# Linear attention and block 2's value products from unrounded fp32 operands, both head pairs at once, and weights in units of four tiles

## Chip, cores and metric

One core of one Trainium2 chip runs the whole program. The metric is the device time of one execution in microseconds (us); lower is better. TensorE is called PE (PEld is its weight load), VectorE DVE, ScalarE ACT, GpSimd POOL and SyncE SP.

## The reference

Two transformer blocks run one after the other on x of 512 positions by 1024 channels, all in fp32. Cut to what matters:

```python
# block 1: block attention (8 heads of 64) and differential attention (4 heads), gates, feed-forward
merged = sigmoid(ga) * (ya @ w_branch_a) + sigmoid(gb) * (yb @ w_branch_b)
x = x + rms_norm(merged @ w_out, g)
f = (silu(h @ w_gate) * (h @ w_up)) @ w_down          # 2816 wide

# block 2: linear attention with decay (4 heads, keys 64, values 128) beside 8 dilated heads of 64
b = cumsum(log_a)                                     # per chunk of 64
scores = einsum('bhik,bhjk,bhijk->bhij', q, k, exp(b_i - b_j))   # causal
o = (q * exp(b)) @ state + scores @ v
state = state * exp(b_last) + (k * exp(b_last - b)).T @ v
p = softmax(q @ k.T / 8 + bias);  y = p @ v           # dilated heads
x = x + g1 * (concat(rms_norm(o) * silu(r), y) @ w_out)
x = x + g2 * ((silu(conv(h @ w_up)) * conv(h @ w_up)) @ w_down)
```

Before the first line of block 2, a modulation vector is made from `w_ada` (48 tiles of 128 by 1024).

## The kernel before, in words

**Products.** Activations lie transposed, 128 channels by 512 positions. A weight tile is 128 by 128; there are 1760. Full precision comes from three products of rounded operands (type fp32r): each operand is split into a rounded high part and the rounded rest, and `mm3` adds high-high, high-low and low-high. Weights are split on the chip: `_raw` starts the transfer of eight tiles (128x1024) on SP into one of two buffers `wraw`, `_split` makes `whi` (a cast, on ACT or DVE) and `wlo` (a subtraction, on DVE) from a half of it, four tiles, and asks for the next transfer; `wt` hands out tiles and splits up to three halves ahead. A buffer is free once both its halves are split.

**Order.** A planner (`Rec`) holds a model of the costs of all engines, places every operation at its modelled time, and `play` emits them in that order; so every operation has the line of `play` (L311). On each engine the order is fixed: an operation that waits holds all that stand behind it. `either` lets the planner choose between two engines (`copy`: ACT or DVE; `both` and `aside`: DVE or POOL). `pump` mixes tasks (attention heads, norms) with dense work (projection tiles, `mtile`): a task that can go is taken first, dense work fills, and some dense work is held back until a head is done (`d_qk`, `d_gr`).

**Stages in the order of time.** Block 1's projections and attention (`block1_mix`) to about 320 us; there `e_b` evacuates branch b: a product into `gb`, the add of both branches into x, the split. Then `block1_rest`: a bridge over `w_out`, the gate and up products (`e_gate`, `e_up`: `g`, `sg`, `u`, `ah`, `al`), with `modulate` beside them: POOL starts the transfer of a tile of `w_ada` into one of two buffers, DVE multiplies and sums it (`junk`). Per gate and up pair two or three of these are done. Then the bridge over `w_down`, `block2_mix`, a bridge over `w_out2`, and block 2's feed-forward.

**Linear attention** (`gla`, for a pair p of heads). The decay is factored over levels: for distances below 128 seven levels (64 to 1), `near`, each an exponential `E` and products of E with k and q, put into zero-padded operands `pad` (high and low parts of both), four blocks of 128 by 128 on PE, and a predicated copy into the scores `A`. Distances of 128 and 256 are `far`. `turn` makes the probabilities' parts `pth` and `ptl` of a block, and `av` multiplies them with the values' parts. The resource `gla` lets one pair in at a time. `dilated` does a dilated head: scores, softmax, transposes, `att_v`.

## Time and profile before

| | |
|---|---|
| median of 3 runs | 1486.25 us (1485.28 to 1488.97) |
| the profiled execution | 1485.08 us; its span 1483.3 us |
| PE, DVE, ACT, POOL busy | 1417.5, 967.2, 674.5, 117.8 us |
| mean granted PE clock | 0.987 |
| transfers | 220 of 512 KB for weights, 48 of 512 KB for `w_ada` |

The span runs from the first to the last instruction of the profiled execution; launch and end lie around it. A busy time is a sum over an engine's instructions; an idle time is put down to what ended it. The granted clock is 1 at 2.4 GHz and 0.5 at 1.2 GHz. A true fp32 product is two matmul rows in the trace, a rounded one and a transpose one.

### The profile page before, as it was taken

What the parts mean: (1) busy time and instruction counts of PE and PEld (TensorE: products, weight loads), DVE (VectorE), ACT (ScalarE), POOL (GpSimd) and SP (SyncE); (2) the same over time, 40 slices, a digit from 0 to 9 for tenths busy, and PEclk for the clock granted to TensorE, in tenths of its full rate; (3) what the DMA queues carried; (4) which work ended last, traced back from release to release, by engine and by line L of the source; (5) the groups of instructions that cost most, each with busy time, mean ns of one, the idle gap of its engine ahead of it and who ended that gap; (6) DMA issues with size and microseconds to landing.
All of it is one profiled execution on the core that took longest, in us unless ns stands there. A gap on an engine that the chain in (4) does not pass through costs nothing.

```text
span 1483.3 us, 19294 instructions
## 1 busy us (share of the span) xinstructions
PE 1417.5 (96%) x7168; PEld 1183.1 (80%) x7168; DVE 967.2 (65%) x1906; ACT 674.5 (45%) x1333; POOL 117.8 (8%) x152
## 2 busy tenths in 40 slices
PE   8999999999999888899999999889999999999999
PEld 6888888877988666688899777768798788888887
DVE  7877766765775665562457688866866777776322
ACT  5665555543533222232335566756547344443221
POOL 0100000000110110000004012111000000000000
PEclk9999999999999999999999999899999999999999
DMA  4222222335235554533334111122332334433432
GB/s 171 71 72 71 73 84 86 86 107 163 86 91 180 181 172 160 197 114 101 91 122 133 53 58 53 33 65 70 94 110 61 102 112 128 128 88 112 121 114 64
DMA packets 44894, 154.89 MB, mean 104 GB/s; under 512 B 5104, under 2 KB 5760, under 8 KB 44800
## 3 DMA queue, kind: packets, MB, share of 16 engines
q1 hardware_dynamic: 36464, 124.16, 27.2%
q0 software_dynamic: 8192, 29.36, 6.6%
q8 instruction: 56, 0.92, 0.3%
q14 instruction: 38, 0.31, 0.1%
q10 hardware_dynamic: 144, 0.14, 0.0%
HBM read 149.45 MB, written 4.19 MB: 104 GB/s over the span
## 4 chain that ended last, share of the span: by engine, by line
PE 78%; DVE 9%; DMA 5%; ACT 4%; issue 3%; POOL 0%; SPq 0%; ACTq 0%; DVEq 0%; POOLq 0%
PE mm L311 62%; PE s L311 8%; DMA wraw<-w 5%; PE y L311 3%; PE pt L311 3%; PE pc L311 1%; DVE junk L311 1%; DVE wlo L311 1%; DVE u L311 1%; ACT ah L311 1%; DVE E L311 1%; DVE p L311 1%; ACT whi L311 1%; ACT E L311 0%; DVE hl L311 0%
## 5 line engine op out<-in xcount | busy, mean ns | idle before, releaser
L311 PE MATMUL mm<-hh,whi 128*128 128x512 f32 x1096 | 438.9, 400 | 24.7 <-DVE u L311 13.6
L311 PE MATMUL mm<-hh,wlo 128*128 128x512 f32 x1096 | 431.2, 393 | 12.8 <-DVE wlo L311 12.8
L311 PE MATMUL mm<-hl,whi 128*128 128x512 f32 x1096 | 429.5, 392 | 0.0
L311 DVE TENSOR_TENSOR wlo<-wraw,whi 128x512 fp32r<-128x512 f32 x401 | 272.3, 692 | 202.0 <-ACT whi L311 191.6
L311 ACT CAST whi<-wraw 128x512 fp32r<-128x512 f32 x358 | 217.7, 619 | 363.2 <-PE mm L311 172.7
L311 PEld LDWEIGHTS mm<-hh,whi 128*128 128x128 f32 x1096 | 207.3, 189 | 69.2 <-ACT whi L311 17.7
L311 PEld LDWEIGHTS mm<-hh,wlo 128*128 128x128 f32 x1096 | 207.2, 189 | 63.3 <-DVE wlo L311 18.9
L311 PEld LDWEIGHTS mm<-hl,whi 128*128 128x128 f32 x1096 | 207.6, 189 | 39.4 <-DVE hl L311 0.5
L311 PE MATMUL mm<-ah,whi 128*128 128x512 f32 (+1 forms) x296 | 111.9, 378 | 0.1
L311 PE MATMUL mm<-al,whi 128*128 128x512 f32 (+1 forms) x296 | 111.8, 378 | 0.0
L311 PE MATMUL mm<-ah,wlo 128*128 128x512 f32 (+1 forms) x296 | 111.8, 378 | 0.0
L311 DVE SCALAR_TENSOR_TENSOR junk<-p,p 128x1024 bf16<-128x1024 f32 x48 | 58.7, 1222 | 8.9 <-DMA p<-w_ada 8.4
L311 PEld LDWEIGHTS mm<-ah,whi 128*128 128x128 f32 x296 | 55.7, 188 | 10.7 <-DVE u L311 0.5
L311 PEld LDWEIGHTS mm<-al,whi 128*128 128x128 f32 x296 | 55.7, 188 | 10.3
L311 PEld LDWEIGHTS mm<-ah,wlo 128*128 128x128 f32 x296 | 55.7, 188 | 10.3
L311 POOL TENSOR_TENSOR rr<-rv,mhalf 128x4 f32<-128x4 f32 (+2 forms) x26 | 31.5, 1210 | 404.4 <-DVE rv L311 404.4
L311 POOL DMA_DIRECT2D p<-w_ada x48 | 26.1, 543 | 414.6 <-DVE junk L311 346.6
L311 DVE TENSOR_TENSOR ptl<-pt,pth 128x256 fp32r<-128x256 f32 (+3 forms) x92 | 42.3, 479 | 23.7 <-ACT pth L311 22.2
L311 ACT ACTIVATE p<-p,nm 128x128 f32<-128x128 f32 (+1 forms) x96 | 52.8, 552 | 6.7 <-DVE nm L311 6.6
L311 ACT CAST pth<-pt 128x256 fp32r<-128x256 f32 (+3 forms) x84 | 32.6, 412 | 45.7 <-PE pt L311 45.7
L311 DVE CUSTOM_DVE_ANT_0 p<-s,bias 128x128 f32<-128x128 f32 (+1 forms) x96 | 44.4, 488 | 7.4 <-PE s L311 6.3
L311 ACT ACTIVATE sg<-g 128x512 f32<-128x512 f32 x22 | 13.9, 632 | 56.6 <-DVE g L311 56.6
(498 smaller groups left out, 2407.5 us busy)
## 6 DMA issues: line engine op xcount, KB each, us to landing
wraw<-w SPq DMA_DIRECT2D x220, 512.0 KB, 3.6
p<-w_ada POOLq DMA_DIRECT2D x48, 512.0 KB, 4.6
x<-xT SPq DMA_DIRECT2D x8, 256.0 KB, 5.5
x<-xT POOLq DMA_DIRECT2D x8, 256.0 KB, 3.1
xd<-x SPq DMA_DIRECT2D x8, 256.0 KB, 4.5
x<-xd POOLq DMA_DIRECT2D x8, 256.0 KB, 3.0
outT<-x SPq DMA_DIRECT2D x7, 256.0 KB, 2.7
p<-c SPq DMA_DIRECT2D x2, 512.0 KB, 3.9
```

What stands on the lines that cost most here:

```text
L311: i = getattr(getattr(nc, eng), op)(*(real(v) for v in a), **{k: real(v) for k, v in kw.items()})
```

## The change

Weights come in units of four tiles (256 KB) into four buffers; each unit is split by itself and asks for the fourth unit after it. In block 2 the values are kept unrounded (`v_whole`), the probabilities too (`att_whole`, `turn`), and the near and far products take one fp32 product for three rounded ones; E is multiplied straight into the padded operands, for which each pair of heads has its own set; both pairs may be in `gla` at once, and `calm` holds a near step back while the planner's DVE or ACT lane is full more than 2 us ahead. The near products' multiplications by q, and those of `far`, may go to POOL. The heads of block 1 stay as they were. The planner now counts 310 and not 380 GB/s for a transfer; the add in `e_b` may go to POOL (`aside`); a bridge without ready columns begins with the banks `s`; the lambda load of block 1 is issued no earlier than its turn, and block 1's first squares come after the splits. The first four units are asked for between the tiles of x. The rest of the diff is names of tiles and sizes.

```diff
 NTILES = 976 + 784
-NCHUNK = -(-NTILES // 8)
+NHALF = NTILES // 4
+NRAW = 4
...
+CALM = 2.0
...
+PTB = 2
+EB = 3
+VB = 2
...
-            return (0.6 if eng == "gpsimd" else 0.43), b / 380e3, ()
+            return (0.6 if eng == "gpsimd" else 0.43), b / 310e3, ()
...
-        self.limit = 2 * NCHUNK
-        self.res = {"prob": 3, "pv": 1, "gla": 1, "sc": 1, "sq": 1, "v": 1}
+        self.limit = NHALF
+        self.res = {"prob": 3, "pv": 1, "gla": 2, "sc": 1, "sq": 1, "v": 1}
...
+    def calm(self, *vs):
+        n = self.when(*vs)
+        n.calm = True
+        return n
...
-        return max([t.ready] + [self.bank_at(b) for b in t.banks])
+        w = max([t.ready] + [self.bank_at(b) for b in t.banks])
+        if t.calm:
+            w = max(w, *(self.nc.lane[n].end() - CALM for n in ("vector", "scalar")))
+        return w
...
-    def _raw(self, c):
-        if c < NCHUNK and c not in self.raws:
-            raw = self.t(self.wp, [128, 1024], F32, "wraw", 2)
-            self.nc.sync.dma_start(out=raw, in_=self.a["w"][c])
-            self.raws[c] = raw
+    def _raw(self, h):
+        if h < NHALF and h not in self.raws:
+            raw = self.t(self.wp, [128, 512], F32, "wraw", NRAW)
+            self.nc.sync.dma_start(out=raw, in_=self.a["w"][h])
+            self.raws[h] = raw
     def _split(self, h):
-        c, half = divmod(h, 2)
-        if c >= NCHUNK or h in self.chunks:
+        if h >= NHALF or h in self.chunks:
             return
-        self._raw(c)
-        raw = self.raws[c][:, 512 * half:512 * half + 512]
+        self._raw(h)
+        raw = self.raws[h]
         if h in self.keep:
             w = self.keep.pop(h)
             hi, lo = self.hpair(w) if isinstance(w, int) else (self.W(*t) for t in w)
         self.copy(hi, raw)
         self.sub(lo, raw, hi)
         self.chunks[h] = (hi, lo)
-        self._raw(c + 1)
+        self._raw(h + NRAW)
...
+    def v_whole(self, ps, dst):
+        v32 = self.W("v32", F32, 1)
+        self.copy(v32, ps)
+        def go():
+            yield self.when("pt", v32)
+            pt = self.bank("pt")
+            for tb in range(TB):
+                bl = slice(128 * tb, 128 * tb + 128)
+                self.tr(pt[:, bl], v32[:, bl])
+            self.copy(dst, pt)
+            self.res["v"] += 1
+            return self.at(dst)
+        return go()
...
+    def att_whole(self, p, v, cols, y):
+        parts = []
+        def turn(j):
+            pt = self.bank("pt")
+            qs = slice(128 * j, 512)
+            for i in range(j, TB):
+                self.tr(pt[:, 128 * i:128 * (i + 1)], p[:, OFF[i] + 128 * j:OFF[i] + 128 * (j + 1)])
+            ph = self.W("pt", F32, PTB)
+            self.copy(ph[:, qs], pt[:, qs])
+            parts.append(ph)
+        for j in range(2):
+            yield self.when("pt", p)
+            turn(j)
+        for j in range(TB):
+            qs = slice(128 * j, 512)
+            yield self.when(v, parts[j][:, qs])
+            self.mm(y[:, qs], v[:, 128 * j + cols.start:128 * j + cols.stop], parts[j][:, qs], j == 0, j == TB - 1)
+            if j + 2 < TB:
+                yield self.when("pt", p)
+                turn(j + 2)
...
-                nc.vector.tensor_tensor(out=ga, in0=ga, in1=g, op=ALU.add)
+                self.aside(out=ga, in0=ga, in1=g, op=ALU.add)
                 mg[m] = self.split(ga, [T(*t) for t in mgt[2 * m:2 * m + 2]])
...
             def f(ps):
-                dst = (X(2 * hd, F32R), X(2 * hd + 1, F32R)) if hd < 2 else None
-                gv[hd], g = self.v_parts(ps, dst=dst)
-                self.add(g, gvd[hd])
+                gv[hd] = X(hd)
+                self.add(self.v_whole(ps, gv[hd]), gvd[hd])
             return f
...
-            def decayed(s):
+            def decays(s):
                 n = 512 // (2 * s)
-                cv, qv, kv = (halves(t, s) for t in (cs[max(s, 64)], q, k))
-                e = T("E", F32, 2)
+                cv = halves(cs[max(s, 64)], s)
+                e = T("E", F32, EB)
                 ev = halves(e, s)
                 ref = cv[:, :, 0, s - 1:s].to_broadcast([128, n, s])
                 self.both("tensor_tensor", out=ev[:, :, 0], in0=ref, in1=cv[:, :, 0], op=ALU.subtract)
                 if s >= 64:
-                    self.copy(ev[:, :, 1], cv[:, :, 1])
+                    nc.scalar.activation(ev[:, :, 1], cv[:, :, 1], AF.Exp, scale=1.0 / 16.0)
+                    nc.scalar.activation(ev[:, :, 0], ev[:, :, 0], AF.Exp, scale=1.0 / 16.0)
                 else:
                     self.both("tensor_tensor", out=ev[:, :, 1], in0=cv[:, :, 1], in1=ref, op=ALU.subtract)
-                nc.scalar.activation(e, e, AF.Exp, scale=1.0 / 16.0)
-                self.both("tensor_tensor", out=ev[:, :, 0], in0=ev[:, :, 0], in1=kv[:, :, 0], op=ALU.mult)
-                nc.vector.tensor_tensor(out=ev[:, :, 1], in0=ev[:, :, 1], in1=qv[:, :, 1], op=ALU.mult)
+                    nc.scalar.activation(e, e, AF.Exp, scale=1.0 / 16.0)
                 return e
...
+            def far(s, tag):
+                ev, qv, kv = (halves(t, s) for t in (decays(s), q, k))
+                t = T(tag)
+                xv = halves(t, s)
+                self.both("tensor_tensor", out=xv[:, :, 0], in0=ev[:, :, 0], in1=kv[:, :, 0], op=ALU.mult)
+                self.both("tensor_tensor", out=xv[:, :, 1], in0=ev[:, :, 1], in1=qv[:, :, 1], op=ALU.mult)
+                return t
...
             def near(s, b):
...
+                e = decays(s)
+                kt, qt = padk[p][b], pad[p][b]
+                self.both("tensor_tensor", out=halves(kt, s)[:, :, 0], in0=halves(e, s)[:, :, 0],
+                          in1=halves(k, s)[:, :, 0], op=ALU.mult)
                 for hd in range(2):
                     own = slice(64 * hd, 64 * hd + 64)
...
+                    eq, qq = (t[own].rearrange("p (i n h s) -> p i n h s", i=TB, h=2, s=s)[:, :, :, 1]
+                              for t in (e, q))
+                    self.both("tensor_tensor", out=qt[own].rearrange("p (i e n s) -> p i e n s", i=TB, e=2, s=s)[:, :, hd],
+                              in0=eq, in1=qq, op=ALU.mult)
+                return kt, qt
+            def prod(ps, t, e, kc, qc):
                 own = slice(64 * e, 64 * e + 64)
-                self.mm3(ps, [t[own, kc] for t in xx], [pick(t[own]) for t in xx], first, True)
...
+                self.mm(ps, t[own, kc], t[own, qc], True, True)
+            yield self.calm()
             xx = near(LEVELS[0], 0)
...
             for li, s in enumerate(LEVELS):
+                yield self.calm()
                 nxt = near(LEVELS[li + 1], (li + 1) % 2) if li < 6 else None
                 if li >= 5:
-                    if p:
-                        yield glad[1]
-                    big.append(far((128, 256)[li - 5], f"yah{li - 3}", f"yal{li - 3}"))
+                    yield self.calm()
+                    big.append(far((128, 256)[li - 5], ("yah%d", "yal%d")[li - 5] % (2 + p)))
...
-                    self.mm3(ps[:, bl], [t[:, bl] for t in xx[:2]], [t[:, bl] for t in xx[2:]])
+                    self.mm(ps[:, bl], xx[0][:, bl], xx[1][:, bl], True, True)
                 mk = lmask[:, li].rearrange("p (n h s) -> p n h s", h=2, s=s)[:, :, 1].unsqueeze(1)
                 for e in range(2):
+                    if li == 0:
+                        self.copy(A[e][:64].rearrange("p (i h s) -> p i h s", i=TB, h=2)[:, :, 1],
+                                  ps[:64].rearrange("p (i e s) -> p i e s", i=TB, e=2)[:, :, e])
+                        continue
                     nc.vector.copy_predicated(
...
                 def turn(j):
-                    ph, pl = T("pth", F32R, 2), T("ptl", F32R, 2)
-                    d = slice(128 * j, 128 * j + 128)
-                    self.copy(ph[:, d], A[e][:, d])
-                    self.sub(pl[:, d], A[e][:, d], ph[:, d])
+                    ph = None
                     if j < 3:
                         ps = self.bank("pt")
+                        d = slice(128 * j, 128 * j + 128)
                         if j % 2 == 0:
                             nx = slice(128 * j + 128, 128 * j + 256)
-                            prod(ps[:, nx], X1, e, d, lambda t: t[:, nx], True)
+                            prod(ps[:, nx], X1, e, d, nx)
                         if j < 2:
-                            prod(ps[:, 256:512], X2, e, d, lambda t: t[:, 256:512], True)
+                            prod(ps[:, 256:512], X2, e, d, slice(256, 512))
                         o = slice(128 * j + 128, 512)
-                        self.copy(ph[:, o], ps[:, o])
-                        self.sub(pl[:, o], ps[:, o], ph[:, o])
-                    parts.append((ph, pl))
+                        t = T("pt", F32, PTB)
+                        if j == 0:
+                            self.copy(t[:, :128], A[e][:, :128])
+                        self.copy(t[:, o], ps[:, o])
+                        ph = t if j == 0 else t[:, o]
+                    parts.append(ph)
                 for j in range(2):
-                    yield self.when("pt", *X1, *X2)
+                    yield self.when("pt", X1, X2)
                     turn(j)
                 for j in range(TB):
-                    yield self.when(*gv[hd], *(t[:, 128 * j:512] for t in parts[j]))
-                    self.av(y, j, gv[hd], slice(0, 128), *parts[j])
+                    d = slice(128 * j, 128 * j + 128)
+                    yield self.when(gv[hd], A[e], *([] if j == 3 else [parts[j]]))
+                    if j == 0:
+                        self.mm(y, gv[hd][:, d], parts[j], True, False)
+                    else:
+                        self.mm(y[:, d], gv[hd][:, d], A[e][:, d], False, j == 3)
+                        if j < 3:
...
         def e_av(box):
             def f(ps):
-                box["v"], g = self.v_parts(ps)
-                self.add(g, box["vd"])
+                box["v"] = T("vt", F32, VB)
+                self.add(self.v_whole(ps, box["v"]), box["vd"])
...
-            yield from self.att_v(p, box["v"], slice(64 * e, 64 * e + 64), y[:64])
+            yield from self.att_whole(p, box["v"], slice(64 * e, 64 * e + 64), y[:64])
```

DVE, in the gate and up products: the `wlo` of two transfers with what stands between them (`wraw_1062` is one transfer of eight tiles; `p1` and `p2` hold `w_ada`). Before:

```order
L311 TENSOR_TENSOR wlo_1069_4642<-wraw_1062_4609,whi_1068_4637 128x512
L311 TENSOR_TENSOR u_1071_4653<-mm_1065_4604,g_1063_4614 128x512
L311 TENSOR_TENSOR al5_1073_4663<-u_1071_4653,ah5_1072_4659 128x512
L311 SCALAR_TENSOR_TENSOR junk_1015_4263,mod_8_4264<-p2_1074_4599,p0_1013_2972 128x1024
L311 SCALAR_TENSOR_TENSOR junk_1015_4263,mod_8_4264<-p1_1075_4630,p0_1013_2972 128x1024
L311 TENSOR_TENSOR wlo_1078_4687<-wraw_1062_4609,whi_1077_4649 128x512
L311 TENSOR_TENSOR wlo_1080_4697<-wraw_1070_4644,whi_1079_4672 128x512
L311 TENSOR_TENSOR g_1082_4704<-mm_1076_4651,rbc_988_4314 128x512
```

And of the change, at the same kind of place; a `wraw` is four tiles:

```order
L323 TENSOR_TENSOR wlo_1184_4979<-wraw_1163_4879,whi_1183_4949 128x512
L323 TENSOR_TENSOR u_1186_4987<-mm_1179_4925,g_1177_4955 128x512
L323 TENSOR_TENSOR al7_1188_5001<-u_1186_4987,ah7_1187_4994 128x512
L323 SCALAR_TENSOR_TENSOR junk_1081_4391,mod_8_4392<-p1_1189_4929,p0_1079_3056 128x1024
L323 SCALAR_TENSOR_TENSOR junk_1081_4391,mod_8_4392<-p2_1190_4958,p0_1079_3056 128x1024
L323 TENSOR_TENSOR wlo_1193_5025<-wraw_1173_4937,whi_1192_4970 128x512
L323 TENSOR_TENSOR wlo_1196_5032<-wraw_1176_4942,whi_1195_4999 128x512
```

Before, the two halves of a transfer are split with `u`, `al` and two `junk` between them; in the change every `wlo` has a transfer of its own, and the operations around it stand as they did.

PE, in block 2, where dilated heads (`tk`, `kl`, `tq`; transposes of `p`) meet the end of linear attention. Before, this is a piece of 70 rows without a weight product:

```order
L311 MATMUL s_1886_8876<-tk0_1822_8643,tq0_1769_8353 128x384
L311 MATMUL s_1886_8876<-kl_1823_8657,tq0_1769_8353 128x384
L311 MATMUL s_1887_8882<-tk0_1822_8643,tq0_1769_8353 128x512
L311 MATMUL s_1887_8882<-kl_1823_8657,tq0_1769_8353 128x512
L311 MATMUL s_1894_8891<-tk1_1824_8678,tq1_1770_8362 128x128
L311 MATMUL s_1894_8891<-kl_1825_8683,tq1_1770_8362 128x128
L311 MATMUL pt_1896_8898<-ident_3_78,p2_1752_8384 128x128 x4
L311 MATMUL pt_1899_8911<-ident_3_78,p2_1752_8384 128x128 x3
L311 MATMUL s_1902_8924<-tk1_1824_8678,tq1_1770_8362 128x256
L311 MATMUL s_1902_8924<-kl_1825_8683,tq1_1770_8362 128x256
```

And of the change, where the last near products (`pad`, `padk`) meet a dilated head; `whi` and `wlo` are weight products:

```order
L323 MATMUL mm_1986_8750<-hh3_1679_7394,whi_1913_8503 128x512
L323 MATMUL mm_1986_8750<-hl3_1680_7403,whi_1913_8503 128x512
L323 MATMUL mm_1986_8750<-hh3_1679_7394,wlo_1914_8509 128x512
L323 MATMUL s_1996_8800<-pad2_1736_7508,padk2_1740_7676 128x128 x4
L323 MATMUL pt_1998_8812<-ident_3_78,p0_1935_8602 128x128 x4
L323 MATMUL pt_2000_8817<-ident_3_78,p0_1935_8602 128x128 x3
L323 MATMUL s_2002_8828<-tk1_1906_8474,tq1_1868_8335 128x512
L323 MATMUL s_2002_8828<-kl_1907_8490,tq1_1868_8335 128x512
L323 MATMUL mm_1986_8750<-hh4_1681_7428,whi_1918_8507 128x512
L323 MATMUL mm_1986_8750<-hl4_1682_7436,whi_1918_8507 128x512
L323 MATMUL mm_1986_8750<-hh4_1681_7428,wlo_1919_8515 128x512
L323 MATMUL y_1997_8839<-pt_1999_8825,vt_1897_8556 64x512
```

Weight products (`mm`) now stand between the heads' steps; the longest piece without one has 29 rows in this stage. A near product of a level is one row of four, where before it was twelve.

DVE, in branch b of block 1: `gb` is the product with the gate, `tq0` and `tq1` take the low part of the sum x. Before:

```order
L311 TENSOR_TENSOR gb0_494_1950<-gb0_494_1950,mm_795_3233 128x512
L311 TENSOR_TENSOR x0_110_396<-x0_110_396,gb0_494_1950 128x512
L311 TENSOR_TENSOR tq0_799_3272<-x0_110_396,tq0_798_3265 128x512
L311 TENSOR_TENSOR wlo_802_3279<-wraw_794_3210,whi_801_3270 128x512
L311 TENSOR_TENSOR gb1_569_2240<-gb1_569_2240,mm_800_3254 128x512
L311 TENSOR_TENSOR x1_202_735<-x1_202_735,gb1_569_2240 128x512
```

And of the change:

```order
L323 TENSOR_TENSOR gb0_522_2004<-gb0_522_2004,mm_843_3329 128x512
L323 TENSOR_TENSOR tq0_848_3372<-x0_118_410,tq0_847_3366 128x512
L323 TENSOR_TENSOR wlo_851_3378<-wraw_834_3285,whi_850_3359 128x512
L323 TENSOR_TENSOR gb1_601_2302<-gb1_601_2302,mm_849_3350 128x512
L323 TENSOR_TENSOR gb2_609_2357<-gb2_609_2357,mm_855_3369 128x512
L323 TENSOR_TENSOR tq1_854_3410<-x1_201_714,tq1_853_3404 128x512
```

The add into x has left DVE for POOL, and two `gb` stand ahead of the second subtraction.

## Rows read from the trace of the kernel before

**Rows 1.** The page's first part: busy us (share of the span) and instructions.
```profile
PE 1417.5 (96%) x7168; PEld 1183.1 (80%) x7168; DVE 967.2 (65%) x1906; ACT 674.5 (45%) x1333; POOL 117.8 (8%) x152
```
**Rows 2.** Busy time by stage: window, its length, busy us (instructions), clock, DMA share, GB/s.
```profile
320.00:368.00 48.00, 44.38 (x180) 34.92 (x179) 29.19 (x46) 19.21 (x33) 4.90 (x9) 0.93 0.51 150
440.00:480.00 40.00, 40.00 (x179) 33.10 (x178) 25.08 (x41) 12.26 (x21) 3.77 (x7) 1.00 0.58 191
480.00:640.00 160.00, 136.15 (x572) 105.20 (x571) 96.55 (x157) 41.66 (x73) 15.59 (x29) 1.00 0.52 174
...
840.00:940.00 100.00, 93.14 (x523) 78.95 (x522) 83.24 (x213) 66.36 (x147) 21.34 (x21) 0.97 0.16 48
940.00:980.00 40.00, 30.14 (x139) 23.59 (x139) 34.10 (x84) 29.67 (x66) 2.19 (x3) 0.79 0.16 45
980.00:1060.00 80.00, 79.71 (x443) 66.12 (x442) 58.27 (x136) 47.71 (x107) 12.42 (x12) 1.00 0.25 74
1060.00:1080.00 20.00, 17.32 (x89) 11.96 (x88) 13.95 (x31) 10.41 (x26) 0.53 (x1) 1.00 0.39 120
```
**Rows 3.** Who waited for whom, PE, 480 to 640: us in total, times, longest.
```profile
PE mm L311 <- DVE u L311: 13.6, 12, 1.8
PE mm L311 <- DVE wlo L311: 10.3, 12, 0.9
```
**Rows 4.** The chain that ended last, 470 to 500: start, us, what.
```profile
472.15 6.64 DMA wraw<-w
...
478.89 0.63 ACT whi L311
...
479.54 0.04 DVE wlo L311
...
484.62 0.61 DVE wlo L311
...
485.29 6.86 DMA wraw<-w
```
**Rows 5.** Landing of `wraw` from 440 to 640, and the page's issues of `x<-xd`.
```profile
DMA to landing us min/median/max: 3.6/5.2/7.6
...
x<-xd POOLq DMA_DIRECT2D x8, 256.0 KB, 3.0
```
**Rows 6.** The DMA view, 4 to 12 us: GB/s in 40 equal slices.
```profile
GB/s 338 423 333 349 307 348 317 307 317 287 318 338 440 369 410 348 451 389 481 389 389 420 471 307 389 389 369 389 420 379 420 399 410 410 389 420 394 364 451 405
```
**Rows 7.** PE's timeline, three windows: start, us, instructions (the fp32 ones s<-A,c).
```profile
830.59 1.02 PE L311 MATMUL s<-A,c 16*128 16x512 f32 x2
...
831.02 1.02 PE L311 MATMUL s<-A,c 16*128 16x512 f32 x2
...
880.32 0.95 PE L311 MATMUL s<-pad,pad 128*128 128x128 f32 x7
```
**Rows 8.** Groups of DVE and ACT, 838 to 1080: busy us, mean ns | idle before.
```profile
L311 DVE TENSOR_TENSOR pad<-E,pad 64x256 fp32r<-64x256 f32 x28 | 11.7, 417 | 0.7
L311 DVE TENSOR_TENSOR ptl<-pt,pth 128x384 fp32r<-128x384 f32 x12 | 6.6, 551 | 1.8 <-ACT pth L311 1.8
...
L311 ACT CAST pad<-E 64x256 fp32r<-64x256 f32 x28 | 11.4, 409 | 1.1 <-DVE E L311 0.8
```
**Rows 9.** PE's timeline, 946 to 976, three rows with idle time before them.
```profile
947.83 0.45 PE L311 MATMUL y<-ptl,vh 128*64 128x512 f32 x1 [0.65 <-DVE ptl L311]
...
955.79 2.79 PE L311 MATMUL s<-pad,pad 128*128 128x128 f32 x12 [3.02 <-ACT E L311]
...
975.28 0.33 PE L311 MATMUL y<-ptl,vh 128*64 128x256 f32 x1 [0.92 <-DVE ptl L311]
```
**Rows 10.** PE's waits from 318 to 350, and two groups of POOL.
```profile
PE mm L311 <- DVE gb L311: 3.6, 4, 2.3
...
L311 POOL DMA_DIRECT2D x<-xT x8 | 4.4, 546 | 47.5 <-DVE tq L311 30.5 <-DVE tk L311 6.0 <-DVE vl L311 2.8
...
L311 POOL TENSOR_TENSOR E<-gq,gk 128x512 f32<-128x512 f32 x1 | 1.7, 1653 | 0.4 <-DVE yal L311 0.4
```

More of the change, by code (lines that the diff above doesn't have):

```diff
@@ L141, in clash, with end @@
         return None
+    def end(self):
+        return self.e[-1] if self.e else 0.0
     def put(self, t, d):
@@ L462, in mm3, with add @@
         self.mm(out, l[1], r[0], False, last)
-    def add(self, gen, done=None):
-        self.tasks.append(Task(gen, done))
+    def add(self, gen, done=None, rank=0):
+        self.tasks.append(Task(gen, done, rank=rank))
+        self.tasks.sort(key=lambda t: t.rank)
     def dense(self, gen, gate=None):
@@ L494, in _step @@
             return True
-        t.banks = ()
+        t.banks, t.calm = (), False
         if isinstance(r, Done):
@@ L1610, in gla_norm @@
             yield glad[3]
-            yg[hd] = self.split(o, [T(f"pad{i}{hd % 2}", F32R) for i in ((0, 1) if hd < 2 else (2, 3))])
+            yg[hd] = self.split(o, [T(t, F32R) for t in (f"pad{hd}", f"padk{hd}")])
         def qk_norm(w, f, box, done):
```

66 lines of the change are left out of this document (27 added, 39 removed).

## Prediction

> **What bounds the kernel now.** I read the page's first part, then the busy time by stage, then the waits and the chain of the two stages that lose time, and last the single prices. TensorE is busy for 96% of the span [rows 1], so only two things help: less TensorE work, or closing the places where it waits or runs at the low clock. The stages show where these are [rows 2]. From 440 to 480 us PE runs without a gap: 179 matmuls in 40 us, 0.2235 us each, so four weight tiles (12 matmuls) take 2.68 us. By that price the 572 matmuls from 480 to 640 need 128 us and take 160: the feed-forward of block 1 loses 32 us. From 840 to 1080, the attention of block 2, PE is idle for 6.9 + 9.9 + 0.3 + 2.7 = 19.7 us, and the granted clock averages 0.97 for 100 us and 0.79 for 40 us. With levels of 2.4 and 1.2 GHz that is 6 + 17 us at the low one, worth up to 11 us more. So about 31 us are lost there, and 18 of them stand between 940 and 980. VectorE is busy for 190 of these 240 us, 85% from 940 to 980, and ScalarE for 154. From 320 to 368 3.6 us are idle and the clock is 0.93.
>
> **Why the feed-forward loses 32 us.** PE waits there for DVE: for `u`, which frees a bank, and for `wlo` [rows 3]. The chain of waits says why [rows 4]. A weight transfer of eight tiles is issued at 472.15 and lands 6.6 us later; its first half is split at 479.5, its second only at 484.6, since `u`, `al` and two `junk` operations stand between them on DVE; only then is the buffer free and the next transfer issued, at 485.29. One turn is 13.1 us, and in a turn the two buffers carry one pair of gate and up (16 tiles), for which PE needs 48 x 0.2235 = 10.7 us. The order of before shows the same thing: two `wlo` of one `wraw` with four operations between. The stage is bound by the turn of a buffer, not by bytes.
>
> **The change, part by part.**
>
> *Units of four tiles.* Each half is now its own buffer, asked for again as soon as its own `wlo` is done. The order of the change has each `wlo` on a `wraw` of its own. Four buffers serve four halves a pair, so a buffer turns once in 10.7 us, and a turn costs the landing (3.6 to 7.6 us for 512 KB in this stage [rows 5], no more for half the bytes) plus a cast of 0.6 and a split of 0.6 [rows 4]: at most 8.8. That fits. Bytes fit too: a pair moves 1.05 MB of weights and 1.3 MB of `w_ada`, 220 GB/s at full pace. The stage before moves 191 with no loss [rows 2], and the start of the kernel far more [rows 6]. DVE has 96.6 us for 12 pairs [rows 2], 8 of each 10.7. What is late next is a `junk` whose `w_ada` has not landed, with the next `wlo` behind it on DVE; the three halves split ahead cover 8 us of that. I leave 0.6 us a pair for it: **-25 us**. Below it is all 32; above, if half the stall only changes its name, -14. Elsewhere PE shows no weight wait to speak of, so the other 300 units earn nothing; the 220 extra issues lie on SP, which does nothing else.
>
> *TensorE work in block 2.* A true fp32 product of 512 columns is two matmul rows 0.43 us apart (830.59 and 831.02), 0.86 in all; three rounded ones are 3 x 0.2235 = 0.67. For 128 columns the rounded row costs 0.11 (7 in 0.95 us, the last with its latency) [rows 7], and the fp32 product by columns 0.215. The near products go from 168 rows to 56 products: 18.8 to 12.0 us, -6.8. The 16 far products, 128 and 256 columns: from 5.4 to 5.2. The value products have 1280 columns a head: three passes 1.68, fp32 2.15 us, so +0.47 for each of 12 heads, +5.6 us; in the four linear-attention heads the three rounded rows of 128 columns cost 0.11 and not 0.056, so 0.7 less. Sum **-2 us**; the ends are -4 (if that holds for the 64-wide heads and the far products too) and 0.
>
> *DVE and ACT work in block 2.* Gone are the subtractions of the near operands (28 in 11.7 us, and 14 more of that width, 5.9), those of the probabilities (`ptl`: 12 of 384 columns in 6.6, with 12 each of 128 and 256 and eight of 512 about 19 by columns, and 16 of 128 for `A`, 3) and six of 512 of the values, 4: together about 44 us of DVE [rows 8]; 42 casts of the near operands (28 in 11.4, so 17 us) leave ACT. The products with q and k are the same number of operations as before, now written straight into the padded operands. None of this is on PE; it is worth what PE waits there. So the order decides. In the kernel before, PE has up to 70 rows in a row without a weight product, and they fall between 947 and 976, where the profile has the hole [rows 9]; with both head pairs let in at once the longest such stretch of the change is 29 rows, and weight products stand between the chain's steps. I take 16 of the hole's 18 us, and 4 of the other 13, which are waits at the start of the chain and after the last weights, where nothing can fill: **-20 us**. Ends: -31, and -5 if the chain's own latencies make the hole rather than the load.
>
> *The add of branch b moves from DVE to POOL.* From 318 to 350 PE waits 3.6 us for `gb`, which stands behind an add, a subtraction and a split on DVE. On POOL an fp32 operation of 512 columns took 1.65 us, and POOL issues the reload of x behind it, 0.55 [rows 10]. Add, cast 0.6, subtraction 0.7, issue: 3.5 us a tile against PE's 2.68. POOL falls behind by 0.8 a tile; the order gives room, two `gb` ahead of the first subtraction, but the subtractions hold the `wlo` behind them, and near the end these come late. **-2 us**, ends -6 and +4.
>
> *The rest:* a first unit of half the size lets the first x land earlier, by at most 0.7 us; banks `s` first in a bridge, the later squares, the place of the lambda load, and the copy in place of one predicated copy have no price that PE sees. **-1 us**.
>
> Sum: -25 - 2 - 20 - 2 - 1 = -50 against the profiled execution's 1485.1, 1435; the median of the runs is 1.2 above that execution, so **1436**.
>
> **Rivals.**
> *A, the forecast:* both holes mostly close. Its own range is 1424 to 1448. Chance 0.60.
> *B, the feed-forward stays half:* `w_ada` and weights share the engines, PE runs faster, and DVE stands before `junk` instead of `wlo`. For it: two buffers of `w_ada` and their junks on the in-order DVE; against it: 191 GB/s without a loss. 1436 + 11 = 1447. Chance 0.15.
> *C, block 2 stays:* its waits are the latency of each near step (exponential, product, copy), and a lighter DVE shortens only the queueing. For it: the longest wait of PE there, 3.0 us, is for an exponential [rows 9]. 1436 + 15 = 1451. Chance 0.13.
> *D, slower:* small transfers do not overlap on SP's queue. A transfer of 256 KB lands in 3.0 us [rows 5]; one after the other, 440 units would come 0.3 us slower than PE eats them: 1485 + 440 x 0.32 = 1626. It decides once a unit takes more than 2.68 us. Against it: with x coming in units of 256 KB at the start, the engines move 287 to 481 GB/s in every slice [rows 6], which singles of 3.0 us (87 GB/s) cannot. Chance 0.02.
> The Trainium skill's page "DMA: Bandwidth & Descriptors" speaks against this part of the change: its section "Rules for kernel authors" asks for at least 1 MiB per DMA, and "Anatomy of one DMA — SWDGE (gpsimd) path" gives about 2.0 us fixed plus the bytes over 436 GB/s. By that, an estimate, 512 KB take 3.2 us and 256 KB 2.6, so half units one at a time would just keep pace with PE and not slow it; the trace has 3.6 at best and 3.0, so it agrees that halving the bytes saves little of a landing.
> *E, better:* both stages run clean and block 2 loses only its start: 1415. Chance 0.07.
> *F, nothing:* an operation that the planner prices too low holds DVE or POOL in order and gives it all back: 1485. Chance 0.03.
>
> **How the numbers follow.** The forecast is A's. Its range is widened to E below and to B and C with their spread above: **1414 to 1458**. A measurement of this kernel can tell some 0.3%, 4.5 us, from no change. A, B, C and E are faster: 0.95. F is the same: 0.03. D is slower: 0.02.
>
> **What would show it.** In the feed-forward, PE gets through its 12 pairs in about 135 us, ACT hardly waits for `wraw`, and the turn of 13.1 us is gone; if DVE waits for `w_ada` instead and PE still loses 10 us, it is B. In block 2 the clock stays near 1.00 and PE's idle time falls below 10 us; DVE's busy time there falls by about 44 us. If that fall is there and the idle time is not, it is C. PE's near products should be two rows each, about 0.11 apart. In branch b, PE should wait less than 3.6 us for `gb`, and late `wlo` should show at the bridge. The prediction is wrong if weight transfers land later than 7.6 us in the feed-forward, or if the fp32 rows cost more than 0.43 us per 512 columns.

## The result, and the profile after

The changed kernel takes 1423.96 us (median of 4 runs, 1422.38 to 1425.37), the kernel before on the same chip 1487.61: a ratio of 0.9573, 95% interval 0.9554 to 0.9592. The span of the profiled execution fell from 1483.3 to 1423.5 us, by 59.8. The page's first part, beside [rows 1]:

```profile
PE 1399.1 (98%) x7064; PEld 1164.1 (82%) x7064; DVE 920.0 (65%) x1780; ACT 657.1 (46%) x1274; POOL 141.4 (10%) x179
```

Since the stages begin at other times now, they are compared from one operation to the same one: the feed-forward of block 1 from its first `g` to the first product of `w_down` in a bank `mm` (in the change six matmuls of `w_down` go to banks `s` just before, 1.4 us that are counted to the feed-forward), block 2's attention from the end of the gate products to the first residual of `w_out2`. Of before, busy time by stage (columns as in [rows 2]):

```profile
422.90:668.90 246.00, 221.10 (x945) 175.19 (x944) 151.13 (x245) 71.40 (x121) 19.36 (x36) 1.00 0.50 162
822.90:1087.90 265.00, 245.31 (x1301) 198.12 (x1300) 201.46 (x478) 164.19 (x360) 36.48 (x37) 0.95 0.21 63
```

And of after, with two stretches of the start ahead and one of the last feed-forward behind:

```profile
24.00:28.00 4.00, 2.52 (x18) 2.22 (x17) 0.99 (x3) 0.62 (x1) 1.14 (x1) 0.95 0.21 70
28.00:32.00 4.00, 4.00 (x13) 3.13 (x12) 3.22 (x6) 1.56 (x3) 0.00 (x0) 0.62 0.00 0
...
419.60:636.30 216.70, 215.64 (x952) 178.23 (x951) 151.15 (x246) 75.36 (x123) 19.36 (x36) 1.00 0.57 186
...
790.50:1027.00 236.50, 235.61 (x1197) 178.31 (x1197) 161.35 (x367) 139.75 (x299) 50.31 (x56) 1.00 0.25 72
...
1090.00:1110.00 20.00, 19.86 (x76) 16.20 (x77) 13.38 (x20) 7.23 (x12) 0.00 (x0) 0.85 0.28 92
```

Read the second number (length) less the third (PE busy): that is PE's idle time. The feed-forward lost 24.9 us and loses 1.1. Block 2 lost 19.7 and loses 0.9, and its clock is 1.00, where a mean of 0.95 had cost about 10 us (an estimate: PE's busy time times 1 - clock, summed over windows of 0.5 us; time in which PE idles costs nothing more at the low clock). DVE has 40 us less to do there, ACT 24 less, POOL 14 more. By stage the 59.8 us are:

| stretch | change, us | forecast |
|---|---|---|
| start, to branch b | +1.9 | part of -1 |
| branch b and the bridge over `w_out` | -5.2 | -2 |
| feed-forward of block 1 | -29.3 | -25 |
| bridge over `w_down`, gates | +0.2 | 0 |
| attention of block 2 | -28.5 | -22 (-2 and -20) |
| bridge over `w_out2`, last feed-forward | +1.1 | 0 |

The largest of PE's waits in the whole of after (us in total, times, longest):

```profile
PE mm L323 <- ACT hh L323: 6.8, 3, 5.3
PE mm L323 <- DVE cg L323: 4.0, 1, 4.0
PE mm L323 <- DVE hl L323: 1.7, 3, 0.8
PE pt L323 <- POOL rr L323: 1.5, 1, 1.5
PE mm L323 <- ACT p L323: 1.4, 1, 1.4
PE mm L323 <- ACT al L323: 1.4, 1, 1.4
PE mm L323 <- DVE wlo L323: 1.1, 1, 1.1
```

`u` and `wlo` of [rows 3], `gb` of [rows 10], `E` and `ptl` of [rows 9] are gone but for three `wlo` (this one, and two of 1.0 us together outside the feed-forward). What is left is mainly the start (`hh`, `rr`) and the 4.0 us for `cg` where the last feed-forward begins, which the kernel before has too.

### The profile page after: what moved, and what is told of

It is laid out like the page before. It is cut to its first block, busy times and chain, and to the rows that moved or that the text cites. A ratio compares the mean times of both kernels' runs of the same rounds, so it can differ in the third digit from the quotient of the medians.

```text
span 1423.5 us, 19514 instructions
## 1 busy us (share of the span) xinstructions
PE 1399.1 (98%) x7064; PEld 1164.1 (82%) x7064; DVE 920.0 (65%) x1780; ACT 657.1 (46%) x1274; POOL 141.4 (10%) x179
## 4 chain that ended last, share of the span: by engine, by line
PE 90%; issue 3%; DVE 3%; ACT 2%; POOL 1%; DMA 0%; DVEq 0%; POOLq 0%; ACTq 0%
PE mm L323 72%; PE s L323 8%; PE y L323 4%; PE pt L323 4%; PE pc L323 2%; POOL x L323 1%; ACT p L323 0%; DVE hl L323 0%; DVE cg L323 0%; ACT hh L323 0%; DVE cv L323 0%; ACT ah L323 0%; DVE al L323 0%; DMA wraw<-w 0%; DVE wlo L323 0%
## 5 line engine op out<-in xcount | busy, mean ns | idle before, releaser
L323 ACT CAST whi<-wraw 128x512 fp32r<-128x512 f32 x358 | 221.3, 620 | 400.6 <-PE mm L323 333.2
L323 DVE TENSOR_TENSOR wlo<-wraw,whi 128x512 fp32r<-128x512 f32 x401 | 269.8, 691 | 146.6 <-ACT whi L323 143.1
L323 DVE SCALAR_TENSOR_TENSOR junk<-p,p 128x1024 bf16<-128x1024 f32 x48 | 58.7, 1222 | 10.7 <-DMA p<-w_ada 10.5
L323 DVE CUSTOM_DVE_ANT_0 p<-s,bias 128x128 f32<-128x128 f32 (+1 forms) x96 | 44.5, 487 | 13.6 <-PE s L323 12.4
L323 DVE SCALAR_TENSOR_TENSOR cv<-mm,vecs,cv 128x511 f32<-128x511 f32 (+1 forms) x40 | 30.0, 750 | 12.6 <-ACT cv L323 11.9
L323 DVE SCALAR_TENSOR_TENSOR cg<-mm,vecs,cg 128x511 f32<-128x511 f32 (+1 forms) x42 | 31.4, 749 | 9.6 <-ACT cg L323 8.9
L323 PEld LDWEIGHTS pt<-ident,p 128*128 128x128 f32 x200 | 24.3, 140 | 14.7 <-issue 9.9
```

The source lines that it names most:

```text
L323: i = getattr(getattr(nc, eng), op)(*(real(v) for v in a), **{k: real(v) for k, v in kw.items()})
```

## Experiments

Each run has its own comparison with the kernel before on its chip. "Stage" is the stretch as above, "idle" its length less PE's busy time, "low clock" what the low clock cost PE, estimated as above.

### What the feed-forward lost

**e1, units of four tiles alone, in the kernel before.** The hunks of the change for `_raw`, `_split` and their limits as shown above, the layout of `w` that goes with them, the first four units asked for between the tiles of x, and nothing else:

```diff
-            raw = self.t(self.wp, [128, 1024], F32, "wraw", 2)
+            raw = self.t(self.wp, [128, 512], F32, "wraw", NRAW)
...
-        self._raw(c + 1)
+        self._raw(h + NRAW)
```

> The kernel before with one part of the change alone: weights in units of four tiles, four buffers, each unit split and asked for again by itself (the first four asked for between the tiles of x). Theory (a buffer was held from the split of its first half to that of its second, a turn of 13.1 us for 10.7 us of work): the feed-forward of block 1, 246 us from the first gate and up product to the first product of w_down in the kernel before, falls to about 216, as in the change; block 2 keeps its 20 us of idle PE. Sum 1486 - 30 = 1456, at most 1460. Rival (the gain of that stage comes from the rest of the change, from the planner's new price of a transfer and the order that it gives): the stage keeps 235 us or more, 1475 to 1486.

1459.29 us, ratio 0.982 (0.9803 to 0.9838). The feed-forward, then block 2:

```profile
421.10:637.70 216.60, 214.96 (x944) 176.70 (x943) 150.54 (x244) 72.08 (x121) 19.35 (x36) 1.00 0.58 184
```
```profile
793.20:1063.60 270.40, 249.94 (x1301) 202.91 (x1300) 203.13 (x480) 166.13 (x363) 36.77 (x37) 0.94 0.21 62
```

The units alone give the gain of the feed-forward, 29.4 us (the change: 29.3, or 30.7 to its first product of `w_down` in any bank), and 2.5 from branch b to it. Block 2 keeps its idle time, 20.5 us. It is also 5.4 us longer than before, with the same code, most of it at the low clock: the planner lays it out anew. Differences of that size in block 2 say little by themselves.

**e2, the hold alone.** Units and buffers of before, both halves of a transfer split one behind the other:

```diff
-            for i in range(h + 1, min(h + 4, self.limit)):
+            for i in range(h + 1, min(h + 4 - (h % 2), self.limit)):
                 self._split(i)
```

> The kernel before, its units of eight tiles and its two buffers, with one line changed: both halves of a transfer are split one behind the other, so that the second doesn't stand behind u, al and junk on DVE (a buffer is read ahead whole or not at all; that leaves two to three halves ahead and not three). Theory (the hold between the two halves is what costs): the turn falls from 13.1 to about 9 us (landing 5 to 7, two casts and splits 2), below the 10.7 us of work, and most of the 31 us goes: 1455 to 1468. Rival (it is the size of a transfer that costs: 512 KB land too late for two buffers, and a 256 KB one lands sooner): nothing, 1483 to 1489.

1471.07 us, ratio 0.9905 (0.9888 to 0.9922): between the two. The feed-forward takes 228.8 us, 17.2 less, with 8.8 idle. The chain that ended last, in it (start, us, what):

```profile
473.86 6.26 DMA wraw<-w
...
481.91 0.04 DVE al L311
...
482.52 1.24 DVE junk L311 x2
483.78 1.23 DVE junk L311 x2
485.01 1.22 DVE wlo L311 x2
...
486.28 5.15 DMA wraw<-w
...
495.10 1.23 DVE junk L311 x2
496.33 1.22 DVE wlo L311 x2
...
497.60 5.02 DMA wraw<-w
```

The two `wlo` now stand together (one row, x2), but `al` and two `junk` still stand ahead of both: the turn is 12.4 and 11.3 us, not the 9 that I expected. The stage has 945 matmuls, 19.7 pairs of gate and up, so a pair takes 11.6 us: about the turn, not PE's 10.7. The hold between the halves was worth 17 of the 29 us; the rest goes when every half returns its own buffer (e1).

**e5, two small buffers for four, in the change.**

```diff
-NRAW = 4
+NRAW = 2
...
-            if k in (1, 3, 5):
+            if k in (1,):
```

> The changed kernel with two buffers of four tiles in place of four: half the bytes in flight, each unit still split by itself. Theory (what counts is the turn of a buffer against the work that it feeds: landing, plus cast and split, plus what stands ahead of them on ACT and DVE): two buffers serve four units a pair of gate and up, 5.3 us a turn; landing is 2.3 to 6.4 us in that stage of the changed kernel and 1.3 go for cast and split, 4 to 8 with the queue on DVE, so the stage loses some 10 to 40 us and the stages without w_ada little: 1434 to 1465. Rival (the size of a unit is what counts, two buffers do as they did before): 1422 to 1427.

1443.58 us, ratio 0.9717 (0.9692 to 0.9742). The feed-forward takes 226.6 us, and other stages lose as well. Landing of `wraw` there, before, e5 and the change:

```profile
DMA to landing us min/median/max: 3.5/5.0/7.6
```
```profile
DMA to landing us min/median/max: 2.4/3.4/7.0
```
```profile
DMA to landing us min/median/max: 2.3/4.0/6.4
```

Small transfers land sooner, soonest where only two are in flight, and yet two buffers are too few. So it is the turn against the work that it feeds, and neither the size nor the landing by itself.

### What block 2 lost

**e3, one pair of heads at a time, in the change.** `-"gla": 2` `+"gla": 1`, nothing else.

> The changed kernel, with one pair of heads at a time in linear attention, as before (unrounded fp32 operands, padded operands of each pair, and units of four tiles stay). Theory of the prediction (the order makes the hole: with one pair at a time there are long pieces without a weight product): PE idles 10 to 20 us in block 2 again and the clock falls there: 1436 to 1452. Rival (the lighter DVE and ACT alone close the hole, the order is worth nothing): PE idle in block 2 below 3 us, 1422 to 1427.

1426.7 us, ratio 0.9608 (0.9595 to 0.9621), block 2:

```profile
790.90:1029.20 238.30, 236.58 (x1197) 178.55 (x1196) 164.64 (x379) 137.07 (x293) 45.17 (x50) 1.00 0.24 71
```

Idle 1.7 us. With one pair at a time, as before, the hole stays closed: the rival won, and letting both pairs in is not what closed it. (The run doesn't bring back the long piece without a weight product, though: its longest takes 7.9 us, the change's 12.3, that of the kernel before 29.2.)

**e6, the subtractions put back, one pair; e7, the same with both pairs.** In the change, DVE does 114 subtractions more (54 us in e6, 52 in e7), on the tiles that stand where the kernel before subtracted, into a scratch tile `scr` that nobody reads:

```diff
             self.copy(ph[:, qs], pt[:, qs])
+            self.load(ph[:, qs])
...
+    def load(self, v, own=slice(0, 128)):
+        n = v.n
+        self.nc.vector.tensor_tensor(out=self.scr[own, :n], in0=v, in1=v, op=ALU.subtract)
```

> The changed kernel with one pair of heads at a time (as in e3) and with the subtractions of before put back on DVE in block 2, about 110 operations on the same tiles at the same places, whose result nobody reads. PE's work and the order's rules stay those of e3. Theory (DVE's queue made the waits of the kernel before in block 2; e3 showed that the order alone does not): DVE in block 2 rises from 165 to about 205 us, PE idles 8 to 20 us there again: 1437 to 1455. Rival (the shorter chain closed the hole: a near step without a cast and a subtraction between exponential and product): the result is not waited for, PE idle stays below 4 us, 1425 to 1432.

> The same put-back subtractions, with both pairs of heads at once, as in the change. With e6 it shows what the order is worth when DVE is as loaded as before. If two pairs at once serve as cover (theory of the prediction): idle of PE at least 6 us less than in e6, 1426 to 1438. If the order is worth nothing under load either: within 3 us of e6.

e6: 1466.75 us, ratio 0.9872 (0.9849 to 0.9895). e7: 1458.54, 0.9812 (0.9784 to 0.984). Block 2 in e6, then in e7:

```profile
789.90:1068.60 278.70, 254.91 (x1197) 191.65 (x1196) 204.56 (x477) 148.66 (x311) 45.52 (x50) 0.90 0.20 60
```
```profile
791.70:1061.50 269.80, 246.93 (x1197) 185.00 (x1196) 201.67 (x471) 148.67 (x316) 50.56 (x50) 0.94 0.21 62
```

And the largest of PE's waits there in e6:

```profile
PE s L323 <- DVE pad L323: 14.3, 6, 2.8
```

The planner moves some casts and copies from DVE to ACT in answer (ACT has 12 and 9 us more), so that DVE's busy time rises by 40 us in both. Block 2 takes 40 us longer in e6 than in e3, and 33 in e7 than in the change. That is more than I expected. In e6 PE waits for `pad`, the operands of the near products, six times between 972 and 997 us. The busy time from 970 to 1000, and a step of the chain that ended last, in it:

```profile
970.00:1000.00 30.00, 15.15 (x61) 13.03 (x59) 26.14 (x68) 8.30 (x19) 3.87 (x6) 0.50 0.02 9
```
```profile
979.41 2.06 PE s L323 x8
...
981.50 0.42 DVE A L323
...
982.17 0.42 DVE scr L323
982.59 0.33 DVE pad L323
982.92 0.34 DVE scr L323
...
983.27 0.43 DVE pad L323
...
983.84 2.06 PE s L323 x8
```

A step takes 4.4 us: 2.1 on PE at the low clock, the rest on DVE, where the put-back work stands between the operations that PE needs (22.5% of this chain from 970 to 1000). (That work also reads `E` and the probabilities' tiles, so it holds those longer: POOL waits 15.8 us for it before it refills an `E`, ACT 5.8. What this adds wasn't taken apart.) In e7 the wait for `pad` is 0.9 us; there PE waits for other results of DVE, `sqh`, `A` and `yah`. Two pairs at once saved 8.9 us of block 2 under load, only 0.9 of it idle time: not the 6 of idle time that the one theory asked for, more than the 3 us of the other, and not far over the 5.4 by which block 2 moved in e1. What the order is worth under load stays open.

**e8, unrounded value products of the dilated heads alone, and e9, unrounded near products alone, in the kernel before.** The hunks of the change for `att_whole` and `e_av`, and those for `near`:

```diff
-            yield from self.att_v(p, box["v"], slice(64 * e, 64 * e + 64), y[:64])
+            yield from self.att_whole(p, box["v"], slice(64 * e, 64 * e + 64), y[:64])
```
```diff
-                    self.mm3(ps[:, bl], [t[:, bl] for t in xx[:2]], [t[:, bl] for t in xx[2:]])
+                    self.mm(ps[:, bl], xx[0][:, bl], xx[1][:, bl], True, True)
```

> The kernel before, with the value products of the eight dilated heads alone from unrounded fp32 operands (40 fewer subtractions of probabilities and values on DVE, some 22 us; linear attention and the units of eight tiles stay). In the changed kernel a row of such a product of 512 columns follows the last by 0.50 us, not by the 0.43 of the prediction, and the eight heads' value products take 22 us in place of some 14. Theory (DVE's load makes the idle time of block 2): PE's work +8, idle and low clock -10 to -16: 1476 to 1486. Rival (the idle is linear attention's own): +8 with nothing back, 1491 to 1497.

> The kernel before with the near products of linear attention alone from unrounded fp32 operands: E times k and q written straight into the padded operands, one fp32 product for three rounded ones (56 for 168 rows), 42 subtractions and 42 casts gone; far products, value products, one pair of heads at a time and the units of eight tiles stay. Theory (the work on DVE and ACT that stood in the chain of the near steps made the hole of block 2; e8 took off DVE work elsewhere and got nothing): PE's work -6, and of the 30 us of idle time and low clock at least 18 go: 1455 to 1464. Rival (only the whole of DVE's load counts, of which this is 17 of 40 us): some 10 of the 30 go: 1467 to 1475. Rival (the hole is none of these): the 6 us of PE's work alone, 1478 to 1482.

e8: 1493.76 us, ratio 1.0052 (1.0031 to 1.0073). e9: 1472.38, 0.9911 (0.9879 to 0.9944). Block 2 in e8, then in e9:

```profile
823.10:1095.50 272.40, 255.13 (x1269) 194.68 (x1268) 188.88 (x452) 162.40 (x353) 35.99 (x35) 0.94 0.20 61
```
```profile
820.60:1073.10 252.50, 234.33 (x1245) 188.53 (x1244) 192.86 (x455) 147.61 (x317) 34.72 (x35) 0.97 0.22 66
```

Each takes 9 to 13 us off DVE, and the idle time hardly moves (17.3 and 18.2 of 19.7). e9 gains PE's own 6 us and a better clock; e8 loses what the fp32 products cost. My theory for e9, that the near steps' own subtractions are what matters, fell. Neither part alone closes the hole: e9 is worth 14 us, e8 less than nothing.

The kernels whose block 2 differs, by DVE's work there, with the longest time that PE goes without a weight product (the longest piece):

| kernel | DVE busy, us | PE idle | low clock | stage | longest piece, us |
|---|---|---|---|---|---|
| the change | 161 | 0.9 | 0 | 236.5 | 12 |
| e3 | 165 | 1.7 | 0 | 238.3 | 8 |
| e11 (below) | 178 | 5.1 | 0 | 231.4 | 9 |
| e8 | 189 | 17.3 | 12 | 272.4 | 24 |
| e9 | 193 | 18.2 | 5 | 252.5 | 28 |
| before | 201 | 19.7 | 10 | 265.0 | 29 |
| e7 | 202 | 22.9 | 9 | 269.8 | 44 |
| e1 | 203 | 20.5 | 15 | 270.4 | 29 |
| e6 | 205 | 23.8 | 17 | 278.7 | 63 |

The idle time goes with DVE's load, whichever subtractions make it and whether one or both pairs are let in, and the low clock comes with it. But the longest piece goes with the load too, and in the six kernels from e8 down about half of the idle time or more lies in it (9.8 us before, 22.4 in e6). The planner places operations by its model of all engines, so a heavier DVE also changes the order that PE is given: in e6 157 matmuls stand in that piece, in e3 47. That the load brings the idle time back is shown (e6, e7); whether by DVE's queue itself or by the order that the planner then makes, these runs don't separate.

### The smaller terms

**e4, the squares of block 1 without their hold of 2 us; e10, the add of branch b on DVE again**, both in the change:

```diff
-                yield Need(self.at(*h[k]) + 2.0, ())
```
```diff
-                self.aside(out=ga, in0=ga, in1=g, op=ALU.add)
+                nc.vector.tensor_tensor(out=ga, in0=ga, in1=g, op=ALU.add)
```

> The changed kernel, without the rule that holds block 1's squares back by 2 us after each split. In the changed kernel the column sums of these squares start at 24.4 us, not at 21.7, PE then waits 1.5 us for rr at 25.3 and runs at the low clock for some 3 us, and by 60 us the program is 1.9 us behind the kernel before though it began 1.3 us ahead of it. Theory (the later squares cost this): the wait and the low clock go, 3 us less, 1421. Rival (the place of the squares is not what sets rr, or the squares now hold up the first splits): 1424 or more.

> The changed kernel with the add of branch b on DVE again. From the first gb to the end of the bridge over w_out the changed kernel gains 5.2 us on the kernel before; e1, with the add on DVE and units of four, gained 2.5 in the same stretch. Theory (the add on POOL is worth the other 2.7): 2 to 4 us slower than the changed kernel on the same chip. Rival (the add is worth nothing, the rest of the change gave it): within 1 us of it.

e4: 1421.24 us, ratio 0.957 (0.9557 to 0.9583), the change's own. By its trace the start is only 0.7 us shorter: the column sums begin at 21.2 us and the wait for `rr` is gone, but PE waits 1.3 us for a `wlo` at 18.9, since seven adds of squares now stand in a row ahead of it on DVE, and the low clock comes all the same. e10: 1426.13 us, ratio 0.9592 (0.9566 to 0.9619), beside 1424.36 of the change on the same chip (e12): not told apart. By the trace PE waits again for `gb`,

```profile
PE mm L323 <- DVE gb L323: 2.0, 3, 1.5
```

and the stretch from branch b to the feed-forward gains 3.9 us on the kernel before, where e12 gains 5.2. By this the add is worth some 1.3 us; it takes POOL 1.30 us a tile, not the 1.65 that the prediction had from another operation.

### A version put together from this

**e11** takes back what costs PE time, as far as DVE bears it, in the change; besides these hunks, the gates' sigmoids wait for the second pair's head sums and block 1's squares are held by 1 us:

```diff
-                box["v"] = T("vt", F32, VB)
-                self.add(self.v_whole(ps, box["v"]), box["vd"])
+                box["v"], g = self.v_parts(ps)
+                self.add(g, box["vd"])
...
-            yield from self.att_whole(p, box["v"], slice(64 * e, 64 * e + 64), y[:64])
+            yield from self.att_v(p, box["v"], slice(64 * e, 64 * e + 64), y[:64])
...
-        self.res = {"prob": 3, "pv": 1, "gla": 2, "sc": 1, "sq": 1, "v": 1}
+        self.res = {"prob": 3, "pv": 1, "gla": 1, "sc": 1, "sq": 1, "v": 1}
```

> A version put together from the runs: the changed kernel with the dilated heads' value products from rounded operands again (three rounded passes for an fp32 one, and their subtractions on DVE), linear attention unrounded, one pair of heads at a time (which frees the tiles for the parts, worth 2 us by e3), the gates' sigmoids after the second pair's head sums, and block 1's squares held back by 1 us and not 2. By e8 the fp32 value products cost PE 4 to 5 us more than the rounded ones. Theory (DVE's load does harm only where it stands in linear attention's chain): the put-back 12 us of DVE stay hidden, -4.6 + 2 - 1: 2 to 5 us faster than the changed kernel on the same chip. Rival (any load of DVE opens the hole again): 8 us slower or more.

> The changed kernel itself, for the comparison with e10 and e11 on one chip: 1422 to 1425.

e11: 1419.29 us (1418.41 to 1420.01), ratio 0.9546 (0.952 to 0.9573). e12, the change: 1424.36 (1420.83 to 1424.95), 0.9577 (0.9549 to 0.9604). Block 2 in e11:

```profile
790.70:1022.10 231.40, 226.27 (x1229) 182.65 (x1228) 177.59 (x397) 142.72 (x306) 51.41 (x55) 1.00 0.25 73
```

PE has 9 us less to do than in the change and idles 4.2 more: 5.1 us gained in block 2, and 5.1 in the medians, the lowest time of any version here. Which of its edits gave how much was not taken apart. Its squares, held by 1 us and not 2, gained nothing.

## Why the prediction was right, and where its reason was not

**The feed-forward (-25, measured -29.3).** The mechanism held: the stage ran at the turn of a buffer (e2), and a unit that returns its own buffer closes it (e1). The size was off by what I left for a late `w_ada`, rival B's mechanism. DVE does wait for `w_ada`, 10.5 us from 440 to 620, and ACT still waits 21.9 us for `wraw` there, where the prediction's sign was that it hardly would; the units split ahead cover both, and PE's one wait in the stage is 1.1 us. The Trainium skill's page "DMA: Bandwidth & Descriptors", section "Rules for kernel authors", asks for at least 1 MiB per DMA for the most bandwidth. The measurement decides otherwise for this stage, which was not short of bandwidth: units of 256 KB moved 186 GB/s where units of 512 KB moved 162. Halving the bytes took 1.1 us off the best landing and 1.0 to 1.6 off the median (change, e5), where the prediction's estimate beside rival D has 0.6; that one is for transfers that POOL issues, and these are issued by SP.

**DVE and ACT in block 2 (-20, measured about -29: 18.8 of idle time, 10 of low clock).** Here the step "So the order decides" failed in its cause: both pairs let in at once. One pair at a time is as good (e3), and the load put back brings the idle time back with either (e6, e7). The long pieces without a weight product, which the prediction counted as 70 rows against 29, are where much of the idle time lies; but they are long or short with DVE's load, not with the number of pairs (8 and 63 us with one pair, 12 and 44 with both). So the -20, split by this step into 16 of the hole's 18 us and 4 of the other 13, came near for a reason that was in part wrong. Rival C fell by the prediction's own sign: DVE's load fell, and the idle time with it. Its mechanism is not excluded where the load is high, since most of e6's waits stand in a chain of near steps. What I had called waits "where nothing can fill" closed as well: all of the 19.7 us of idle time but 0.9, and all of the low clock. The load that goes was forecast at 44 us on DVE and 17 on ACT; it was 40 and 24.

**TensorE work in block 2 (-2, measured about +1).** The stage less its idle time and low clock is 235 us before and 236 after. The near products are nearly as forecast (two rows each, sixteen rows in 1.95 us below, 0.11 apart; e9 has 6 us less work, forecast 6.8). The mis-sized price is that of the dilated heads' value products: 3.8 us by the forecast, 8 by e8 and 9 by e11 against the change. PE's timeline of after:

```profile
899.67 1.07 PE L323 MATMUL y<-pt,vt 128*64 128x512 f32 x2
900.67 0.44 PE L323 MATMUL pt<-ident,p 128*128 128x128 f32 x2
901.04 0.86 PE L323 MATMUL y<-pt,vt 128*64 128x384 f32 x2
901.83 0.33 PE L323 MATMUL pt<-ident,p 128*128 128x128 f32 x1
902.09 0.65 PE L323 MATMUL y<-pt,vt 128*64 128x256 f32 x2
902.66 0.65 PE L323 MATMUL pt<-ident,rr 128*128 128x128 f32 x4
903.24 0.43 PE L323 MATMUL y<-pt,vt 128*64 128x128 f32 x2
903.61 0.65 PE L323 MATMUL pt<-ident,rr 128*128 128x128 f32 x4
...
906.84 1.95 PE L323 MATMUL s<-pad,padk 128*128 128x128 f32 x16
```

From the start of each product to the row behind it: 1.00, 0.79, 0.57 and 0.37 us, 2.73 a head. The prediction had 0.86, 0.65, 0.43 and 0.22 by columns, 2.15: each product, alone between transposes, costs 0.14 to 0.16 more than its columns. For 32 products that is 4.6 us. Rounded products cost more than their columns too, but less (the twelve rows of the head at 859.40 in e11 take 1.81 us, forecast 1.68), and the transposes of `p` between fp32 products take longer (10.0 us in the change, 7.2 in e11). Against this miss of 4 to 6 us, linear attention's own value and far products cost less than forecast; that part was not taken apart. The trace of before could have told that fp32 rows cost more than 0.43 each: [rows 7] are the inner rows of a run of four, and the whole run

```profile
830.06 1.98 PE L311 MATMUL s<-A,c 16*128 16x512 f32 x4
831.97 0.50 PE L311 MATMUL mm<-hh,whi 128*128 128x512 f32 x1
```

takes 1.91 us to the row behind it, not 4 x 0.43 = 1.72. A higher price of the fp32 rows was named as a thing that would make the prediction wrong; it came, and was worth some 5 us of 60.

**Branch b and its bridge (-2, measured -5.2).** The add gave about 1.3 (e10); 2.5 came from the units (e1), which I had priced at nothing outside the feed-forward. The rest was not taken apart.

**The rest (-1, measured +3).** PE begins 1.3 us earlier in the change and 0.7 in e12, forecast at most 0.7. But the squares that I had priced at nothing set `rr`: PE waits 1.5 us for it and then runs at the low clock (24 to 32 us in the table of after). Neither the place of before (e4) nor half the hold (e11) mended it; what would is open. At the end PE waits 4.0 us for `cg` as before, but the 20 us behind it have a clock of 0.85, 3 us lost (before: 0.91, just under 2).

So the span fell by 10 us more than the sum of -50: the two holes closed wholly and the units helped branch b too, 17 us more than forecast, and 7 went back to the value products, the start and the low clock behind the wait for `cg`. The time lies at the lower edge of A's own range, but the gain in block 2 did not come from letting both pairs in, by which the prediction had split its 20 us; that the total still fell inside the range is luck in part.

## What to carry to other kernels

Where an in-order engine both returns a transfer's buffer and does other work, compare the turn of the buffer (landing, queue, last read) with the work that it feeds; a unit should return its buffer with its own last read. Where PE idles in a stage full of short dependent steps, sum the helper engine's work in that stage beside reading the order: operations whose result nobody waits for, 54 us of them on DVE, cost 40 us here. And when a lighter helper has closed the hole, ask which of the lightening edits still pays for its price on PE: taking one back gave 5 us more.

## What the runs showed of the hardware

A true fp32 row costs 0.43 us per 512 columns inside a run of its kind ([rows 7]), and a product that stands alone between transposes 0.14 to 0.16 more, whatever its width from 128 to 512 columns (the four above); in a run of sixteen near products' rows nothing of it shows, 0.11 a row to the end. The Trainium skill's page "FP8 and Floating Point Precision", section "TensorE Precision Notes", gives four passes for true fp32. At 0.2235 us a pass that is 0.89 us for 512 columns, an estimate by that page; the rows inside a run agree (0.86), and the 0.14 it doesn't mention.

The low clock cost nearly as much as the waits beside it. e6 and e3 have the same 1197 matmuls in block 2. In e6, at a mean granted clock of 0.90, PE idled 23.8 us, and its busy time was 254.9 us where e3 took 236.6 at 1.00: 18 us more. In e11, with 5.1 us of idle time, the clock stayed at 1.00.
